# Expert weights made one burst later, gate copies right behind their products, gate rows loaded five ahead, list prices of 1.7 and 1.8

## The chip, the cores and the metric

The kernel runs on one core of a Trainium2 chip. The metric is device time in microseconds. Before the change the median of 3 runs is 2131.26 us (2128.56 to 2132.33). One more execution was taken with the hardware profiler on; all rows below are of that one.

## The reference

One decoder layer on 256 tokens of width 2048, in float32: a token mixer (RG-LRU and Mamba-2 heads), and then PEER, the channel mixer, where the change lies. Both halves are modulated by six vectors made from `c` and `w_ada`; the sixth, `gate2`, scales the output of PEER.

```
def peer(h, w_q, sub_keys, u_tab, v_tab):
    q = (h @ w_q) as 8 heads x 2 halves x 128
    sub = q . sub_keys                       # 128 keys for each half
    sub_val, sub_idx = top_k(sub, 16)        # for each half
    cand = sub_val[0][:, None] + sub_val[1]  # 16 x 16 sums for each head
    top_val, top_pos = top_k(cand, 16)       # 16 experts of 128 * 128 for each head
    gate = softmax(top_val)
    act = gelu(x . u_tab[expert])
    return sum(gate * act * v_tab[expert])

x = x + gate2 * peer(rms_norm(x) * (1 + scale2) + shift2)
out = rms_norm(x, final_norm_g)
```

Each token picks 128 of 16384 experts. `u_tab` and `v_tab` have 16384 rows of 2048 floats (8 KB).

## The kernel before

The part before about 770 us (projections, scans, output projection) is not touched. PEER is then done in four ways at once, under an order that the program writes out by hand.

**U items.** An expert index is split as j * 128 + i. For j below 100, products with all rows of `u_tab` are made: 25 quads of four j, each in 8 items, so 200 items, numbered 0 to 199 here (`it` in `u_quad`). An item takes one 512 KB load of `u_tab` (tile `raw`, 4 buffers, issued by SP), a copy to float32r on ACT (L149, tile `hl`, 4 buffers), the remainder of that copy on DVE (L158), and 12 matmuls on PE (L1499 to L1501). SP issues the next load of `raw` only when L158 has freed a buffer. The products go to two arrays in DRAM (`ads2`, tile name `ad`).

**Lists.** While the items run, list products (`l_step`, L1426) sort the picks with j below 100 into lists of 32 tokens by 116 places: 16 products for tokens 0 to 127, then `l_dec(0)` and `open_sparse`, then 16 for the other tokens, and `l_dec(1)`. Each product needs one-hot operands that `prep` makes on DVE (L1411 to L1415), at most three products ahead. Then come 32 products `g_step` (L1474), which build dense weights `Wt` for the 28 values of j from 100 up; they need `prep` as well, and two copies from PSUM to `Wt` on ACT (L1483). After `open_sparse` there is one PSUM bank for all of them. Each entry of this list has a price (1.3 for `l_step`, 1.5 for `g_step`); every item pays in 1.0, and an entry is issued when its price is covered (`bg_pay`).

**Sparse quads.** For the lists, 58 quads of 4 x 128 places are done (`v_quad`, L1590). A quad needs 4 gathers of up to 128 rows of `v_tab` (`v_feed`, L1549, up to 1 MB each, into tiles `tk`, `vq`, `vx`: 6 row buffers, 8 later) and 4 gathers of 128 single floats from `ads2` (`w_feed`, L1562, into `lsm`). POOL issues all of them, in order. From the floats `w_make` makes the quad's weights `Wz`: a GELU on ACT (L1576) and three operations on DVE (L1577, L1579, L1580). `tick` is called once an item: it feeds, makes weights, and issues a quad when the quads are behind an even spread to the end.

**Gate rows.** `gate2` takes 64 loads of 256 KB of `w_ada` (L1341, tile `two`, 2 buffers), each added by one DVE operation (L1354, L1356). `gate2_tick` is called at every second item from 22 on, and at every item from 160 on; not between the start of the lists and `open_sparse` (`sq["first"]`).

**The end.** After item 199 come 56 items for the 28 dense j (L454, L456: U side) and 56 items of V (L1690), with the quads spread between them, then two sums over rows, the final norm and the output.

What a tick issues is fixed when the program is built. An engine takes its instructions in that order: a GELU on ACT whose floats have not landed holds every later copy on ACT, and a gate operation on DVE whose load has not landed holds every later L158.

Of the kernel before, what the change touches and what calls it, by code (L numbers as in the profile page):

```python
# [23 lines left out]
JD = 28  # L24
# [39 lines left out]
def hybrid_kernel(ctx, tc, xT, cols, w_ada, w_in, lru_w, w_o1, w_o2, w_q, keys, u_t, v_t, fng, out):  # L64
# [1270 lines left out]
    def gate2_load():  # L1335
        n = gt["ld"]
        gt["ld"] += 1
        if n < 64:
            q, k = divmod(n, 16)
            gt[n] = ads[:, 2 * (n % 2):2 * (n % 2) + 2].rearrange("p a b -> p (a b)")  # L1340
            sp.dma_start(gt[n], w_ada[k * 128:(k + 1) * 128, 5 * D + q * 512:5 * D + (q + 1) * 512])  # L1341

    def gate2_tick():
        n = gt["n"]
        q, k = divmod(n, 16)
        if n >= 64 or sq["first"] or (k == 0 and gt["fin"] < q - 1):
            return
        if n == 0:
            gate2_load()
        gate2_load()  # L1350
# [69 lines left out]
    def l_step(tb, n):  # L1420
# [16 lines left out]
        return l_pe, l_ew, 1.3  # L1437
# [28 lines left out]
    def g_step(n):  # L1466
        P = {}

        def g_pe():
            a, o = gpend.pop(0)  # L1470
            P[0] = pv = gbank()[:, :NG * JD].rearrange("p (t j) -> p t j", t=NG)
            for t in range(NG):
                for i in range(2):
                    pe.matmul(pv[:, t], a[:, t], o[:, t, i], start=(i == 0), stop=(i == 1))  # L1474

        def g_ew():
            if not Wt:
                Wt.extend(pr.tile([128, JD // 2, 256], FT, name="Wt", tag=f"W{b}") for b in range(2))
            if n < 29:
                prep()  # L1480
            for b in range(2):
                j = slice(b * JD // 2, (b + 1) * JD // 2)
                act.activation(Wt[b][:, :, n * NG:(n + 1) * NG].rearrange("p j t -> p t j"), P[0][:, :, j],  # L1483
                               AF.Copy, scale=1.0 / GSCALE)
        return g_pe, g_ew, 1.5
# [5 lines left out]
    def u_quad(n, pay):  # L1491
        ps = [bank((2 * n + tb) % 3) for tb in range(2)]
        for kp in range(8):
# [29 lines left out]
            if it >= 22 and it % 2 == 0 or it >= 160:  # L1523
                gt["slot"] = it
                gate2_tick()
# [43 lines left out]
    def w_make():  # L1569
        q = sq["made"]  # L1570
        if q >= NQD or q > sq["n"] + 1 or sq["w"] < 4 * q + 4 or sq["it"] < wt[q] + 3:
            return
# [9 lines left out]
    def v_quad(q):  # L1582
# [10 lines left out]
        if m == b - 1:  # L1593
            if b == GA:
                for c in range(4):
# [5 lines left out]
    def sparse():  # L1601
# [3 lines left out]
        while sq["made"] <= q:  # L1605
            sq["it"] += 3
# [15 lines left out]
    def open_sparse():  # L1622
        gbk[:] = [3]
        sq.update(on=True, first=False, all=8 * NU - sq["at"] - 1 + 4 * JD)
        for _ in range(6):
            w_feed(1)
            v_feed(1)
# [262 lines left out]
```

## Time and profile before

| | us |
|---|---|
| median of 3 runs | 2131.26 |
| the profiled execution, its own time | 2114.3 |
| its span, first to last instruction | 2112.6 |
| PE busy | 1982.3 (94%) |
| DVE busy | 1416.3 (67%) |
| ACT busy | 895.7 (42%) |
| POOL busy | 764.6 (36%) |
| moved by DMA | 642.20 MB, mean 304 GB/s |

In the rows below a time is in microseconds from the start of the span, "mean ns" is the mean of one instruction, and a bracket behind a row of the timeline is the idle time of the engine just before it, with what ended that. "PEclk" is the granted clock of TensorE, 1.00 at full speed. "DMA share" is the mean busy share of the 16 DMA engines; it comes out a little above 1 where they are all busy. In the time of the lists PE does an item in about 3 us.

### The profile page before, as it was taken

How to read it: one execution, taken by the hardware profiler on the slowest of the kernel's cores; microseconds unless marked ns; L12 is line 12 of the kernel's file. 1: busy time of each engine (PE TensorE's matmuls, PEld its weight loads, DVE VectorE, ACT ScalarE, POOL GpSimd, SP SyncE). 2: the span in 40 equal slices, each digit the busy share in tenths (PEclk: the TensorE clock that was granted, in tenths of full speed). 3: DMA queues.
4: the chain of work that ended last, by engine and by line, in shares of the span. 5: the costliest groups of instructions: out<-in, count | busy, mean ns of one | idle time of the engine just before them, and what ended most of it. 6: DMA issues, size and time to landing. Idle time of an engine off the chain costs nothing. (4 is left out here: it accounts for less than half of the span.)

```text
span 2112.6 us, 33462 instructions
## 1 busy us (share of the span) xinstructions
PE 1982.3 (94%) x12488; PEld 1552.0 (73%) x12488; DVE 1416.3 (67%) x2177; ACT 895.7 (42%) x1364; POOL 764.6 (36%) x637
## 2 busy tenths in 40 slices
PE   7999999999999999999989779888899999999897
PEld 4789999989998898888777555555565766656563
DVE  3368888898878769779979767565533444445444
ACT  3346666677634454444443222323222333333232
POOL 0013344322202110002301545555456666666463
PEclk9999999999999999999999899999999999999899
DMA  9967667777899855677665799999899899989994
GB/s 388 406 228 252 230 228 236 245 262 267 269 323 331 312 175 178 209 235 265 229 227 186 262 371 379 396 328 339 330 369 415 335 420 422 421 302 422 373 419 175
DMA packets 257356, 642.20 MB, mean 304 GB/s; under 512 B 28352, under 2 KB 132976, under 8 KB 230000
## 3 DMA queue, kind: packets, MB, share of 16 engines
q1 hardware_dynamic: 205712, 390.38, 53.3%
q0 software_dynamic: 40832, 215.51, 25.3%
q10 hardware_dynamic: 10640, 34.08, 4.3%
q8 instruction: 100, 1.64, 0.3%
q14 instruction: 72, 0.59, 0.1%
HBM read 650.45 MB, written 17.34 MB: 316 GB/s over the span
## 5 line engine op out<-in xcount | busy, mean ns | idle before, releaser
L149 ACT ACTIVATE hl<-raw 128x1024 fp32r<-128x1024 f32 x554 | 585.1, 1059 | 1038.7 <-PE b L1501 295.1
L158 DVE TENSOR_TENSOR hl<-raw,hl 128x1024 fp32r<-128x1024 f32 x554 | 699.8, 1270 | 134.7 <-ACT hl L149 133.7
L454 PE MATMUL b<-H,hl 128*128 128x512 f32 x1056 | 377.6, 401 | 1.1 <-ACT X L675 1.1
L1499 PE MATMUL b<-hl,H 128*128 128x512 f32 x800 | 326.5, 408 | 0.5 <-ACT X L1505 0.5
L1501 PE MATMUL b<-hl,H 128*128 128x512 f32 x800 | 317.9, 397 | 2.1 <-DVE hl L158 2.1
L1500 PE MATMUL b<-hl,H 128*128 128x512 f32 x800 | 317.6, 397 | 0.0
L1562 POOL DMA_INDIRECT lsm<-ad,X x232 | 267.0, 1151 | 131.0 <-issue 68.8
L456 PE MATMUL b<-H,hl 128*128 128x256 f32 x1056 | 295.6, 280 | 2.4 <-DVE hl L158 2.4
L454 PEld LDWEIGHTS b<-H,hl 128*128 128x128 f32 x1056 | 198.2, 188 | 61.4 <-issue 12.1
L1549 POOL DMA_INDIRECT tk<-in_v_t,X x132 | 155.2, 1176 | 160.9 <-PE b L1590 104.8
L456 PEld LDWEIGHTS b<-H,hl 128*128 128x128 f32 x1056 | 199.2, 189 | 4.0 <-DVE hl L158 3.0
L1499 PEld LDWEIGHTS b<-hl,H 128*128 128x128 f32 x800 | 153.8, 192 | 50.5 <-issue 20.1
L1501 PEld LDWEIGHTS b<-hl,H 128*128 128x128 f32 x800 | 153.6, 192 | 37.6 <-DVE hl L158 3.6
L1500 PEld LDWEIGHTS b<-hl,H 128*128 128x128 f32 x800 | 154.0, 192 | 29.9
L1690 PE MATMUL b<-hl,X 128*128 128x512 f32 x672 | 162.4, 401 | 9.4 <-DVEq L1806 5.7
L1590 PE MATMUL b<-tk,Wz 128*32 128x512 f32 x1056 | 160.2, 616 | 10.5 <-DMA tk<-in_v_t,X 10.5
L1690 PEld LDWEIGHTS b<-hl,X 128*128 128x128 f32 x672 | 128.0, 193 | 50.3 <-issue 18.3
L809 PE MATMUL b<-H,hl 128*128 128x256 f32 x560 | 161.7, 289 | 0.4 <-DVE ggt L466 0.4
L811 PE MATMUL b<-H,hl 128*128 128x256 f32 x560 | 158.4, 283 | 1.3 <-DVE hl L158 1.3
L810 PE MATMUL b<-H,hl 128*128 128x256 f32 x560 | 158.4, 283 | 0.0
L1579 DVE SCALAR_TENSOR_TENSOR lsm<-lsm,LG 128x4 f32<-128x4 f32 x58 | 9.7, 168 | 209.3 <-ACT lsm L1576 209.2
L394 DVE SCALAR_TENSOR_TENSOR adacc<-adr,cact,adacc 128x1024 f32<-128x1024 f32 x90 | 124.3, 1381 | 25.4 <-DMA adr<-in_w_ada 25.3
(383 smaller groups left out, 3340.5 us busy)
## 6 DMA issues: line engine op xcount, KB each, us to landing
raw<-in_u_t SPq DMA_DIRECT2D x228, 512.0 KB, 5.1
raw<-in_w_in SPq DMA_DIRECT2D x146, 512.0 KB, 4.9
adr<-in_w_ada SPq DMA_DIRECT2D x96, 512.0 KB, 5.0
adw<-in_w_ada SPq DMA_DIRECT2D x64, 512.0 KB, 10.2
raw<-in_w_o SPq DMA_DIRECT2D x64, 512.0 KB, 6.0
raw<-in_w_q SPq DMA_DIRECT2D x32, 512.0 KB, 4.5
two<-in_w_ada SPq DMA_DIRECT2D x64, 256.0 KB, 7.3
raw<-in_u_t ACTq DMA_DIRECT2D x28, 512.0 KB, 7.9
```

What stands on the lines that cost most here:

```text
L149: act.activation(t[:, 0], r, AF.Copy)
L158: dve.tensor_sub(t[:, 1], r, t[:, 0].bitcast(FT))
L454: pe.matmul(ps, w[:, 0, c], x[:, k].rearrange("p a b -> p (a b)"), start=(k == first), stop=False, skip_group_check=True)
L456: pe.matmul(ps[:, :256], w[:, 1, c], x[:, k, 0], start=False, stop=(k == 15), skip_group_check=True)
L809: pe.matmul(ps, wh, hT[:, k, 0, :], start=(k == 0), stop=False)
L810: pe.matmul(ps, wh, hT[:, k, 1, :], start=False, stop=False)
L1499: pe.matmul(o, hh, w[:, 0, :, kk], start=(k == 0), stop=False)
L1500: pe.matmul(o, hl_, w[:, 0, :, kk], start=False, stop=False)
L1501: pe.matmul(o, hh, w[:, 1, :, kk], start=False, stop=(k == 15))
L1562: pool.indirect_dma_start(wA[:, n % 32:n % 32 + 1], None, adf[i], bass.IndirectOffsetOnAxis(ap=LW[:, tb, g, m:m + 1], axis=0), bounds_chec ...
L1590: pe.matmul(sb[c][32 * g:32 * g + 32, :], Wz[:, q % NW, g], buf[4 * q + g][:, c * 512:(c + 1) * 512], start=(m == a), stop=(m == b - 1), s ...
L1690: pe.matmul(ob[tb * 2 + c], w[:, i, s], v[:, k, c * 512:(c + 1) * 512], start=(jj == 0 and (i, k) == (0, 0)), stop=(jj == JD - 1 and k == 1))
```

## The change

Five edits.

1. `w_make` makes a quad's weights only when the quad before it has been issued (`q > sq["n"]` in place of `q > sq["n"] + 1`), and not before 6 ticks after their floats were asked for (3 before).
2. `open_sparse` issues 8 gathers of floats first, and then rows and floats in turn, rows first.
3. `g_step` issues the two copies to `Wt` directly behind the products, not one item later.
4. Gate rows get 6 buffers (two in `two`, four in `S0`) and are loaded five ahead. Their ticks go on in the time of the lists, at every fourth item; after it they come at every second item to the end. All 64 are done before `S0` takes the sums of the first 14 quads.
5. Prices: 1.7 for `l_step` (1.3), 1.8 for `g_step` (1.5).

```diff
-            gt[n] = ads[:, 2 * (n % 2):2 * (n % 2) + 2].rearrange("p a b -> p (a b)")
+            i = n % 6
+            gt[n] = (ads[:, 2 * i:2 * i + 2].rearrange("p a b -> p (a b)") if i < 2 else
+                     S0[:, (i - 2) * 512:(i - 1) * 512])
...
-        if n >= 64 or sq["first"] or (k == 0 and gt["fin"] < q - 1):
+        if n >= 64 or (k == 0 and gt["fin"] < q - 1):
             return
-        if n == 0:
+        while gt["ld"] < n + 6:
             gate2_load()
-        gate2_load()
...
-        return l_pe, l_ew, 1.3
+        return l_pe, l_ew, 1.7
...
         def g_pe():
+            if not Wt:
+                Wt.extend(pr.tile([128, JD // 2, 256], FT, name="Wt", tag=f"W{b}") for b in range(2))
             a, o = gpend.pop(0)
-            P[0] = pv = gbank()[:, :NG * JD].rearrange("p (t j) -> p t j", t=NG)
+            pv = gbank()[:, :NG * JD].rearrange("p (t j) -> p t j", t=NG)
             for t in range(NG):
                 for i in range(2):
                     pe.matmul(pv[:, t], a[:, t], o[:, t, i], start=(i == 0), stop=(i == 1))
+            for b in range(2):
+                j = slice(b * JD // 2, (b + 1) * JD // 2)
+                act.activation(Wt[b][:, :, n * NG:(n + 1) * NG].rearrange("p j t -> p t j"), pv[:, :, j],
+                               AF.Copy, scale=1.0 / GSCALE)
...
-        return g_pe, g_ew, 1.5
+        return g_pe, g_ew, 1.8
...
-            if it >= 22 and it % 2 == 0 or it >= 160:
+            if it >= 22 and it % (4 if sq["first"] else 2) == 0:
...
-        if q >= NQD or q > sq["n"] + 1 or sq["w"] < 4 * q + 4 or sq["it"] < wt[q] + 3:
+        if q >= NQD or q > sq["n"] or sq["w"] < 4 * q + 4 or sq["it"] < wt[q] + 6:
...
         sq.update(on=True, first=False, all=8 * NU - sq["at"] - 1 + 4 * JD)
+        w_feed(8)
         for _ in range(6):
+            v_feed(1)
             w_feed(1)
-            v_feed(1)
```

Counted in the built programs, by the item behind which a thing is issued:

| | before | after |
|---|---|---|
| `open_sparse` | 109 | 116 |
| `l_dec(1)` | 132 | 145 |
| gate loads issued by then | 31 of 64 at item 108 | 42 of 64 at item 108 |
| first quad | 115 | 122 |
| quads issued by item 126 | 4 | 2 |
| quads issued by item 200 | 25 | 23 |
| first product of `g_step` | 136 | 149 |
| last product of `g_step` | 182 | after 199 (three together at the end of the U items) |
| last gate operation | 166 | 163 |

On POOL, at `open_sparse`, the order before is as follows: `lsm` is a gather of 128 floats, `tk`, `vq` and `vx` are gathers of rows.

```order
129 L1539 MEMSET vx 128x2048
130 L1562 DMA lsm<-ad_8715,X_8024 128x1
131 L1549 DMA tk<-in_v_t,X_8024 128x2048
132 L1562 DMA lsm<-ad_8715,X_8024 128x1
133 L1549 DMA tk<-in_v_t,X_8024 128x2048
134 L1562 DMA lsm<-ad_8715,X_8024 128x1
135 L1549 DMA tk<-in_v_t,X_8024 128x2048
136 L1562 DMA lsm<-ad_8715,X_8024 128x1
137 L1549 DMA tk<-in_v_t,X_8024 128x2048
```

And after:

```order
129 L1538 MEMSET vx 128x2048
130 L1561 DMA lsm<-ad_8715,X_8024 128x1 x8
131 L1548 DMA tk<-in_v_t,X_8024 128x2048
132 L1561 DMA lsm<-ad_8715,X_8024 128x1
133 L1548 DMA tk<-in_v_t,X_8024 128x2048
134 L1561 DMA lsm<-ad_8715,X_8024 128x1
135 L1548 DMA tk<-in_v_t,X_8024 128x2048
136 L1561 DMA lsm<-ad_8715,X_8024 128x1
137 L1548 DMA tk<-in_v_t,X_8024 128x2048
```

The floats of the first two quads now stand ahead of all rows, where before three gathers of rows stood ahead of the fourth of floats.

On DVE, from the end of `l_dec(0)` to the first weights, before (L1356 is a gate operation, L1411 to L1415 are one `prep`, L1577 to L1580 the weights `Wz`):

```order
1184 L1464 TENSOR_TENSOR LG<-b_10635,LG 128x116
1185 L1356 SCALAR_TENSOR_TENSOR adgx<-two,cact,adgx 128x512
1186 L158 TENSOR_TENSOR hl<-raw,hl 128x1024 x2
1187 L1411 TENSOR_TENSOR two<-lists 128x1024
1188 L1413 TENSOR_TENSOR lists<-lists 128x232
1189 L1415 TENSOR_TENSOR lists<-lists 128x928
1190 L1356 SCALAR_TENSOR_TENSOR adgx<-two,cact,adgx 128x512
1191 L1577 TENSOR_TENSOR Wz<-lsm,LC 128x128
1192 L1579 SCALAR_TENSOR_TENSOR lsm<-lsm,LG 128x4
1193 L1580 TENSOR_TENSOR Wz<-Wz,lsm 128x128
```

And after, with the gate rows partly in `S0`:

```order
1208 L1416 TENSOR_TENSOR lists<-lists 128x928
1209 L1357 SCALAR_TENSOR_TENSOR ohr<-S_8026,cact,ohr 128x512
1210 L158 TENSOR_TENSOR hl<-raw,hl 128x1024 x2
1211 L1412 TENSOR_TENSOR two<-lists 128x1024
1212 L1414 TENSOR_TENSOR lists<-lists 128x232
1213 L1416 TENSOR_TENSOR lists<-lists 128x928
1214 L1357 SCALAR_TENSOR_TENSOR ohr<-S_8026,cact,ohr 128x512
1215 L1576 TENSOR_TENSOR Wz<-lsm,LC 128x128
1216 L1578 SCALAR_TENSOR_TENSOR lsm<-lsm,LG 128x4
1217 L1579 TENSOR_TENSOR Wz<-Wz,lsm 128x128
```

The first weights stood two copies L158 behind `l_dec(0)`; now they stand five behind it.

On ACT, at the end of the program, before (L1576 is the GELU of a quad's floats, L1731 the square root of the final norm, L1722 squares of the sums):

```order
1058 L1722 ACTIVATE b_23063,rf<-H 128x512
1059 L1722 ACTIVATE b_23064,rf<-H 128x512
1060 L1576 ACTIVATE lsm<-lsm 128x4
1061 L1731 ACT_TABLE_LOAD
1062 L1731 ACTIVATE rf<-rf,epsc 128x1
1063 L1737 ACTIVATE H<-H,rf 128x1024
1064 L1722 ACTIVATE b_17410,rf<-H 128x512
```

And after:

```order
1052 L1575 ACTIVATE lsm<-lsm 128x4
1053 L1732 ACT_TABLE_LOAD
1054 L1732 ACTIVATE rf<-rf,epsc 128x1
1055 L1738 ACTIVATE H<-H,rf 128x1024
1056 L1575 ACT_TABLE_LOAD
1057 L1575 ACTIVATE lsm<-lsm 128x4
1058 L1723 ACTIVATE b_17425,rf<-H 128x512
1059 L1723 ACTIVATE b_17426,rf<-H 128x512
1060 L1723 ACTIVATE b_17427,rf<-H 128x512
1061 L1723 ACTIVATE b_17428,rf<-H 128x512
1062 L1732 ACT_TABLE_LOAD
```

The GELU of the last quad moved behind the first final norm, with two more table loads.

## Rows read from the trace of the kernel before

**Rows 1.** Busy time by stretch. The columns are the stretch, its length, the busy time of PE, its weight loads, DVE, ACT and POOL with instruction counts, the granted clock, the DMA share and GB/s.

```profile
1172.00:1210.00 38.00, 25.32 (x143) 18.36 (x145) 23.00 (x43) 10.08 (x13) 26.37 (x24) 0.82 0.79 288
1210.00:1255.00 45.00, 40.85 (x248) 26.69 (x240) 30.49 (x39) 10.28 (x14) 30.00 (x25) 1.00 1.02 391
1255.00:1275.00 20.00, 12.24 (x73) 7.86 (x74) 15.11 (x20) 4.17 (x6) 2.53 (x3) 0.74 0.69 240
1275.00:1370.00 95.00, 84.34 (x576) 56.86 (x576) 63.05 (x102) 27.25 (x47) 54.48 (x46) 0.98 1.03 402
1370.00:1510.00 140.00, 120.27 (x867) 78.11 (x867) 81.71 (x118) 41.81 (x80) 71.61 (x59) 0.95 0.90 328
1510.00:1640.00 130.00, 118.77 (x684) 75.77 (x683) 44.71 (x60) 36.66 (x57) 77.29 (x68) 0.96 1.01 388
...
1125.00:1172.00 47.00, 47.00 (x265) 37.52 (x265) 45.75 (x53) 18.09 (x19) 7.09 (x4) 1.00 0.60 191
...
1680.00:1850.00 170.00, 168.76 (x1072) 117.11 (x1070) 73.97 (x124) 60.50 (x102) 112.36 (x96) 1.00 1.02 421
```

**Rows 2.** Waits of PE between 1175 and 1275: who waited for what, microseconds in total, times, the longest.

```profile
PE b L1426 <- DVE lists L1415: 22.4, 5, 10.0
```

**Rows 3.** The same between 1275 and 1560.

```profile
PE b L1474 <- ACT Wt L1483: 24.9, 13, 3.9
PE b L1474 <- ACT lsm L1576: 5.3, 3, 2.1
...
PE b L1367 <- ACT Wt L1483: 1.6, 1, 1.6
PE b L1367 <- ACT lsm L1576: 1.6, 1, 1.6
```

**Rows 4.** Timeline of ACT and then of DVE and PE behind `open_sparse`.

```profile
1193.76 1.28 ACT L1576 ACT_TABLE_LOAD   x1 [11.95 <-DMA lsm<-ad,X]
...
1195.29 0.17 DVE L1579 SCALAR_TENSOR_TENSOR lsm<-lsm,LG 128x4 f32<-128x4 f32 x1 [11.91 <-ACT lsm L1576]
...
1199.64 0.93 PE L1426 MATMUL b<-lists,two 128*128 128x116 f16 x8 [10.03 <-DVE lists L1415]
```

**Rows 5.** Timeline of POOL at the same place: the first gathers of floats and of rows, the fourth and the sixth of rows.

```profile
1176.62 1.20 POOL L1562 DMA_INDIRECT lsm<-ad,X  x1 [43.81 <-DVE ohr L1461]
1178.13 1.43 POOL L1549 DMA_INDIRECT tk<-in_v_t,X  x1 [0.30 <-issue]
...
1187.59 0.99 POOL L1549 DMA_INDIRECT tk<-in_v_t,X  x1 [0.30 <-issue]
...
1192.79 0.99 POOL L1549 DMA_INDIRECT vx<-in_v_t,X  x1 [0.31 <-issue]
```

**Rows 6.** Timeline around one late gate row: DVE, then ACT, then PE.

```profile
1483.22 0.75 DVE L1356 SCALAR_TENSOR_TENSOR adgx<-two,cact,adgx 128x512 f32<-128x512 f32 x1 [6.77 <-DMA two<-in_w_ada]
...
1496.09 1.06 ACT L149 ACTIVATE hl<-raw 128x1024 fp32r<-128x1024 f32 x1 [5.09 <-DMA raw<-in_u_t]
1497.06 0.54 ACT L1483 ACTIVATE Wt<-b 128x112 f32<-128x112 f32 x2
...
1497.65 0.55 PE L1474 MATMUL b<-ohr,two 128*128 128x28 f16 x16 [3.92 <-ACT Wt L1483]
```

**Rows 7.** Timeline of PE around a wait of 2.07 us, and two matmuls of an item behind it.

```profile
1467.33 0.55 PE L1474 MATMUL b<-ohr,two 128*128 128x28 f16 x16 [2.07 <-ACT lsm L1576]
...
1468.74 0.63 PE L1499 MATMUL b<-hl,H 128*128 128x512 f32 x1
1469.17 0.63 PE L1500 MATMUL b<-hl,H 128*128 128x512 f32 x1
...
1474.46 0.39 PE L1500 MATMUL b<-hl,H 128*128 128x512 f32 x1
1474.69 0.39 PE L1501 MATMUL b<-hl,H 128*128 128x512 f32 x1
```

**Rows 8.** Timeline of PE in the time of the lists: list products two items and one item apart.

```profile
1135.45 0.59 PE L1426 MATMUL b<-lists,two 128*128 128x116 f16 x8
...
1141.42 0.59 PE L1426 MATMUL b<-lists,two 128*128 128x116 f16 x8
...
1144.68 0.59 PE L1426 MATMUL b<-lists,two 128*128 128x116 f16 x8
```

**Rows 9.** Waits of DVE between 1275 and 1560.

```profile
DVE lsm L1579 <- ACT lsm L1576: 46.7, 12, 6.0
...
DVE adgx L1356 <- DMA two<-in_w_ada: 22.0, 8, 6.8
DVE ohr L1356 <- DMA two<-in_w_ada: 11.6, 3, 5.9
```

**Rows 10.** The end of the program: timeline of ACT, and the last quad on PE.

```profile
2089.78 1.28 ACT L1731 ACT_TABLE_LOAD   x1
...
2104.18 0.60 ACT L1722 ACTIVATE b<-H 128x512 f32<-128x512 f32 x1 [0.61 <-DVE H L1719]
2104.71 0.19 ACT L1722 ACTIVATION_READ_ACCUMULATOR b<-H 128x1 f32 x1
2105.39 0.29 ACT L1731 ACTIVATE rf<-rf,epsc 128x1 f32<-128x1 f32 x1 [0.49 <-DVE rf L1730]
...
2097.58 0.62 PE L1590 MATMUL b<-vq,Wz 128*32 128x512 f32 x2 [2.35 <-DMA vq<-in_v_t,X]
```

More of the change, by code (lines that the diff above doesn't have):

```diff
@@ L1466, in g_step @@
     def g_step(n):
-        P = {}
         def g_pe():
+            if not Wt:
+                Wt.extend(pr.tile([128, JD // 2, 256], FT, name="Wt", tag=f"W{b}") for b in range(2))
             a, o = gpend.pop(0)
-            P[0] = pv = gbank()[:, :NG * JD].rearrange("p (t j) -> p t j", t=NG)
+            pv = gbank()[:, :NG * JD].rearrange("p (t j) -> p t j", t=NG)
             for t in range(NG):
@@ L1474, in g_pe @@
                     pe.matmul(pv[:, t], a[:, t], o[:, t, i], start=(i == 0), stop=(i == 1))
+            for b in range(2):
+                j = slice(b * JD // 2, (b + 1) * JD // 2)
+                act.activation(Wt[b][:, :, n * NG:(n + 1) * NG].rearrange("p j t -> p t j"), pv[:, :, j],
+                               AF.Copy, scale=1.0 / GSCALE)
         def g_ew():
-            if not Wt:
-                Wt.extend(pr.tile([128, JD // 2, 256], FT, name="Wt", tag=f"W{b}") for b in range(2))
             if n < 29:
                 prep()
[L1481 to L1484, printed above, removed]
-        return g_pe, g_ew, 1.5
+        return g_pe, g_ew, 1.8
     dram = ctx.enter_context(tc.tile_pool(name="ad", bufs=1, space=bass.MemoryType.DRAM))
@@ L1594, in v_quad @@
             if b == GA:
+                assert gt["n"] == 64
                 for c in range(4):
@@ L1605, in sparse @@
         while sq["made"] <= q:
-            sq["it"] += 3
+            sq["it"] += 6
             w_feed()
```

## Prediction

> **What bounds the kernel now.** I read the busy time by stretch first, then who PE waits for, then timelines where those waits are longest. Up to 1172 PE is hardly ever idle: in 1125 to 1172 it is busy for all 47 us, with the DMA engines at a share of 0.60 [rows 1]. Behind `open_sparse` this turns round: the DMA share goes to 1.02 or 1.03 whenever nothing stands still, and PE gets holes: 25.3 us of 38, 12.2 of 20, 120.3 of 140 [rows 1]. From 1680 to 1850 both are full, PE at 168.8 of 170 and DMA at 1.02 [rows 1]. So from about 1172 to the end two things are at their limit together: PE by its instructions, DMA by its bytes. Neither PE's work nor the bytes change with this edit. A stall costs time only as far as it leaves the DMA engines without work, and this is what I add up.
>
> The stalls have three causes. (a) A GELU waits for its floats. At 1193.76 ACT had been held 11.95 us by the first floats, DVE was held 11.91 us behind it, and PE 10.03 us behind the next `prep` [rows 4]. The fourth gather of floats was issued behind three of rows [rows 5]. It goes on later: DVE waits 46.7 us for GELUs from 1275 to 1560 [rows 9]. (b) A gate operation waits for its load, 33.6 us of DVE in the same stretch [rows 9]. At 1483.22 it had waited 6.77 us; L158 behind it freed a buffer late, so `raw` was late (5.09 us on ACT), and PE stood 3.92 us [rows 6]. (c) A product of `g_step` waits for the copies of the last one, 24.9 us in 13 waits and 5.3 us more behind a GELU [rows 3]: the copies stand behind the split of the next item, and that split waits for the matmuls which PE has just done.
>
> In PE's own waits that is 22.4 us [rows 2] and 33.4 us [rows 3].
>
> **What the change takes away.** (a) With the floats of two quads ahead of all rows, and 6 ticks and one quad of distance, no GELU should find its floats missing; the 10.03 us goes, and the same kind of wait later. (b) With loads five ahead a gate row has about ten items to land, 30 us, against two items before; the DVE waits of 33.6 us go. (c) The copies now run as soon as the products are done, while PE does the next item (2.7 us, below). ACT waits there for 0.55 us of products, after a split that had waited for the same matmuls, so the wait moves behind it and costs nothing while `raw` is in time. If `raw` is late, ACT is held at L149 as before and the next product waits again.
>
> How much time these stalls cost follows from the DMA engines. Taking 1.02 as full, a stretch loses its length times (1.02 - share) / 1.02 [rows 1]:
>
> - 1172 to 1210: 38 x 0.23 / 1.02 = 8.6 us
> - 1255 to 1275: 20 x 0.33 / 1.02 = 6.5 us
> - 1370 to 1510: 140 x 0.12 / 1.02 = 16.5 us
> - 1510 to 1640: 130 x 0.01 / 1.02 = 1.3 us
> - the stretches at 1.02 and 1.03: none
>
> That is 32.9 us of the DMA engines, the most that edits 1 to 3 can bring while the bytes bind. It is less than the 55.8 us of PE waits, since part of those lies under transfers that had to be made anyway.
>
> **What it adds and moves.**
>
> *The later opening.* The list price of 1.7 puts `open_sparse` 7 items later. An item takes 2.71 us and a list product 0.55 (5.97 us for two items and one product, 3.26 us for one of each [rows 8]), so at 1.7 an item is 2.71 + 0.55 / 1.7 = 3.03 us and seven are 21.2 us. PE does useful items in that time; the DMA engines run at 0.60 in place of 1.02 [rows 1] and lose 21.2 x 0.42 / 1.02 = 8.7 us.
>
> *Floats first.* An issue on POOL takes 1.3 us (four of them from 1187.59 to 1192.79 [rows 5]). Eight of floats put the first rows 10.4 us behind the first floats, against 1.5 us before [rows 5]: 8.9 us later, at the share of the list time, 3.7 us. The fourth gather of rows is then issued 10.4 + 3 x 2.6 = 18 us after the start, and the first quad, six items behind (18 us), may wait on it by one landing. That wait is no second loss: the DMA engines are busy in it.
>
> *What remains of the stalls.* I leave a quarter of the 17.8 us from 1370 on, 4.5 us: `raw` still shares the engines with the bursts of rows. Both ends are open here, nothing and all 17.8 us, since no row shows this stretch without late gates and floats. I take a quarter because the timeline [rows 6] leads the largest hole back to a gate row.
>
> *Gate loads.* 42 are out by item 108, where 31 were: 11 x 262 KB = 2.9 MB leave the full stretch for one with room; at the 402 GB/s of 1275 to 1370 [rows 1] that is 7.2 us gained. On SP they stand in front of `raw` by 0.5 us of issue; the burst of six at item 21 lies in a stretch where PE had cover. On DVE one operation of 0.75 us each fourth item joins the lists [rows 6], while a `prep` is needed at 1 / 1.7 of the items in place of 1 / 1.3; that relieves DVE by more than it adds.
>
> *The end of the U items.* Three products of `g_step` come together there, some 3 us of PE with copies between; DMA runs on beside, so 0, and 3 us if it does not.
>
> *The tail.* The last GELU now stands between the two final norms on ACT, with a table load of 1.28 us each way [rows 10]. The first load hides in the wait for the last rows (the last quad starts at 2097.58, after 2.35 us of waiting [rows 10]). The second begins when the squares end, 2104.71 + 0.19 = 2104.9, and ends 1.28 us later at 2106.2, where the square root began at 2105.39 [rows 10]: 0.8 us lost. [...] The row shows a load of 1.28 us with nothing behind it but work, so the sum keeps 0.8.
>
> *The clock.* Behind a PE wait of 2.07 us matmuls are 0.43 us apart instead of 0.23 for some 3 us [rows 7], so short waits cost double on PE. [...]
>
> **The sum.** Lost before 32.9; lost after 8.7 + 3.7 + 4.5 = 16.9; difference 16.0, plus 7.2 of gate loads, less 0.8 at the tail: 22.4 us. The profiled execution would go from 2114.3 to 2091.9 us. The median of the runs is higher, 2131.26, by a factor of 1.008; scaled by it the gain is 22.6 us and the time 2108.7, say 2109 us.
>
> **Rivals.**
>
> *PE's waits are the time (faster by far).* If DMA has more room than the share tells, all 55.8 us of PE waits go [rows 2, 3], with a few us of half clock behind them, say 4: some 60 us, 2071 us. For it: from 1370 to 1510 the share is 0.90 at 328 GB/s, when 1.02 gives 421 later [rows 1]. Against it: 1275 to 1370 is full at 1.03 with PE at 84.3 of 95, so there the bytes came first [rows 1].
>
> *The burst that opens late (slower).* Two more quads are still to be done at item 126, and the stretch from 1680 on has no room on either engine [rows 1]. If the stalls of the middle stay because `raw` and the bursts keep starving each other, then the loss is 8.7 + 3.7 of the opening and 3 for the left-over products, less 7.2: 8 us slower, with the tail 9, so 2140 us. It decides once more than about 28 of the 32.9 us remain. For it: two of the three holes begin with a wait for `raw` or a gate row behind a burst. Against it: the float and gate waits that start them are what is taken away.
>
> *The first wait changes its name (no change).* The 10 us at the opening come back as a wait of the first quad for its rows, the copies are held by late `raw` as often as before, and gain and loss cancel: 2131 us.
>
> **How the numbers follow.** The sum above holds with a chance of 0.66, with its own range of 2095 to 2122 (no stalls left, 4.5 us better; the middle not improved, 13 us worse). PE's waits as the time 0.16; no change 0.08; slower 0.10. A measurement here can tell 0.2%, 4 us, from nothing. The main case and the first rival are faster: 0.82. For 8 in 10 I go down to the first rival, nearly, and up to just beyond no change: 2076 to 2132 us.
>
> **What would show it.** Right: no GELU wait of 12 us on ACT behind `open_sparse`; DVE's waits on gate rows gone; the waits of L1474 on `Wt` down from 24.9 to a few us; the DMA share from the opening to the end of the U items near 1.0 throughout; the U items ending some 20 us earlier. Wrong: a long wait of the first quad on rows, `raw` waits as long as before, or holes of DMA share in the last stretch that were not there. If PE's holes close without the DMA share reaching 1.02, the first rival is right.

## The result, and the profile after

| | before | after |
|---|---|---|
| median, us | 2131.80 (2128.56 to 2132.49, 4 runs) | 2104.36 (2100.41 to 2109.80, 4 runs) |
| ratio to before | 1 | 0.9876 [0.9848, 0.9904] |
| the profiled execution, its own time | 2114.3 | 2109.8 |
| its span | 2112.6 | 2108.1 |

The changed kernel is 27.4 us faster; 2109 us was predicted, 4.6 us above what came. The profiled execution of before ran 17 us below the median of its kernel, so the two traces lie only 4.5 us apart. Both kernels were therefore traced once more (E1 and E5 below), and where a size matters both traces of each are used.

Busy time of the changed kernel in the stretches of [rows 1], same columns:

```profile
1125.00:1172.00 47.00, 47.00 (x254) 37.78 (x253) 44.06 (x52) 18.39 (x20) 7.08 (x4) 1.00 0.67 217
1172.00:1210.00 38.00, 37.72 (x201) 30.29 (x200) 36.05 (x52) 16.14 (x19) 12.00 (x8) 1.00 0.71 229
1210.00:1255.00 45.00, 33.04 (x166) 16.97 (x166) 19.97 (x29) 8.90 (x12) 32.61 (x30) 0.81 0.92 340
1255.00:1275.00 20.00, 20.00 (x120) 12.68 (x119) 15.21 (x20) 4.52 (x6) 14.83 (x12) 1.00 1.03 406
1275.00:1370.00 95.00, 84.75 (x518) 52.55 (x516) 57.23 (x92) 25.42 (x38) 53.77 (x45) 0.95 1.04 402
1370.00:1510.00 140.00, 128.64 (x875) 81.46 (x876) 80.41 (x114) 44.07 (x80) 79.18 (x67) 0.95 0.92 348
1510.00:1640.00 130.00, 115.98 (x803) 73.45 (x798) 57.22 (x84) 39.16 (x72) 77.17 (x64) 0.95 0.98 377
1680.00:1850.00 170.00, 163.57 (x1013) 112.34 (x1015) 72.42 (x122) 57.62 (x97) 106.27 (x93) 0.98 1.02 422
```

The hole of PE at the opening (25.3 busy of 38) is gone. A new one stands 40 us later, in 1210 to 1255: 33.0 of 45, at a granted clock of 0.81. In 1370 to 1510 PE gained 8 us, and the DMA share rose only from 0.90 to 0.92. From 1275 to 1370 the DMA engines are full in both traces, at shares of 1.03 and 1.04 and 402 GB/s: the bytes bind there. In the second trace of before (E1) they were at 0.91 in that stretch.

The new hole is the first quads. Timeline of PE in the changed kernel:

```profile
1219.19 1.89 PE L1589 MATMUL b<-tk,Wz 128*32 128x512 f32 x2 [7.19 <-DMA tk<-in_v_t,X]
1224.22 1.92 PE L1589 MATMUL b<-tk,Wz 128*32 128x512 f32 x2 [3.14 <-DMA tk<-in_v_t,X]
1227.19 1.92 PE L1589 MATMUL b<-tk,Wz 128*32 128x512 f32 x2 [1.06 <-DMA tk<-in_v_t,X]
```

and the GELU that stood 11.95 us in [rows 4], on ACT:

```profile
1209.97 1.28 ACT L1575 ACT_TABLE_LOAD   x1
1211.27 0.20 ACT L1575 ACTIVATE lsm<-lsm 128x4 f32<-128x4 f32 x1
```

No bracket: its floats were there. In their place the first quads wait for rows, 11.4 us in three waits, since these now leave POOL behind eight gathers of floats (in E7, where they do not, the first quad does not wait for rows).

Waits of PE between 1275 and 1560, the view of [rows 3], and then those of DVE, the view of [rows 9], both in the changed kernel:

```profile
PE b L1475 <- ACT Wt L1478: 7.1, 1, 7.1
PE b L1589 <- DMA tk<-in_v_t,X: 5.8, 5, 2.1
PE b L1589 <- DVE Wz L1579: 4.9, 1, 4.9
PE b L1368 <- DVE LG L1465: 3.3, 1, 3.3
```

```profile
DVE lsm L1578 <- ACT lsm L1575: 43.2, 8, 10.6
DVE hl L158 <- ACT hl L149: 39.5, 17, 6.9
```

No gate row is waited for there any more (33.6 us in [rows 9]). DVE still waits 43.2 us for GELUs, where [rows 9] had 46.7. The 13 waits on copies to `Wt` have become one, of 7.1 us. This is what makes it, ACT and then PE:

```profile
1414.01 1.06 ACT L149 ACTIVATE hl<-raw 128x1024 fp32r<-128x1024 f32 x1 [7.73 <-DMA raw<-in_u_t]
1414.97 0.54 ACT L1478 ACTIVATE Wt<-b 128x112 f32<-128x112 f32 x2
...
1415.56 0.58 PE L1475 MATMUL b<-ohr,two 128*128 128x28 f16 x16 [7.07 <-ACT Wt L1478]
```

ACT takes the split of the next item before the copies, and stood 7.73 us for `raw` there. The name of the wait is the copy; its cause is the load. Such waits have grown. ACT waiting for `raw` from 1175 to 1640, before and then changed:

```profile
ACT hl L149 <- DMA raw<-in_u_t: 47.9, 9, 11.4
```

```profile
ACT hl L149 <- DMA raw<-in_u_t: 75.8, 16, 11.7
```

In the second traces it is 58.6 us (E1) and 84.8 us (E5). ACT itself is no limit there (busy for 44.07 and 44.89 of the 140 us from 1370 to 1510 in the two traces of the changed kernel), but the loads are later against the work that needs them than they were.

### The profile page after: what moved, and what is told of

The parts are those of the page before. It is cut to its first block, busy times and chain, and to the rows that moved or that the text cites. A ratio compares the mean times of both kernels' runs of the same rounds, so it can differ in the third digit from the quotient of the medians.

```text
span 2108.1 us, 33475 instructions
## 1 busy us (share of the span) xinstructions
PE 1985.3 (94%) x12488; PEld 1545.1 (73%) x12488; DVE 1421.7 (67%) x2177; ACT 899.1 (43%) x1366; POOL 766.8 (36%) x637
## 5 line engine op out<-in xcount | busy, mean ns | idle before, releaser
L149 ACT ACTIVATE hl<-raw 128x1024 fp32r<-128x1024 f32 x554 | 585.2, 1059 | 1018.7 <-PE b L1500 242.1
L158 DVE TENSOR_TENSOR hl<-raw,hl 128x1024 fp32r<-128x1024 f32 x554 | 703.7, 1276 | 169.7 <-ACT hl L149 141.6
L454 PE MATMUL b<-H,hl 128*128 128x512 f32 x1056 | 378.9, 402 | 1.1 <-ACT X L675 1.1
L1498 PE MATMUL b<-hl,H 128*128 128x512 f32 x800 | 320.6, 401 | 0.9 <-ACT X L1504 0.5
L1500 PE MATMUL b<-hl,H 128*128 128x512 f32 x800 | 312.8, 391 | 2.0 <-DVE hl L158 2.0
L1499 PE MATMUL b<-hl,H 128*128 128x512 f32 x800 | 312.2, 390 | 0.0
L1589 PE MATMUL b<-tk,Wz 128*32 128x512 f32 x1056 | 239.9, 642 | 29.8 <-DMA tk<-in_v_t,X 21.2
L454 PEld LDWEIGHTS b<-H,hl 128*128 128x128 f32 x1056 | 199.1, 188 | 62.2 <-issue 12.8
L1548 POOL DMA_INDIRECT tk<-in_v_t,X x132 | 148.8, 1127 | 162.8 <-PE b L1589 123.8
L1589 PE MATMUL b<-vq,Wz 128*32 128x512 f32 x536 | 195.0, 614 | 4.6 <-DMA vq<-in_v_t,X 4.0
L1498 PEld LDWEIGHTS b<-hl,H 128*128 128x128 f32 x800 | 150.6, 188 | 50.5 <-issue 19.9
L1500 PEld LDWEIGHTS b<-hl,H 128*128 128x128 f32 x800 | 150.5, 188 | 35.7 <-DVE hl L158 2.9
L1499 PEld LDWEIGHTS b<-hl,H 128*128 128x128 f32 x800 | 150.9, 189 | 29.0
L1589 PEld LDWEIGHTS b<-tk,Wz 128*32 128x32 f32 x1056 | 53.3, 116 | 143.1 <-issue 95.5
```

Of the source, the lines that this page charges most:

```text
L149: act.activation(t[:, 0], r, AF.Copy)
L158: dve.tensor_sub(t[:, 1], r, t[:, 0].bitcast(FT))
L454: pe.matmul(ps, w[:, 0, c], x[:, k].rearrange("p a b -> p (a b)"), start=(k == first), stop=False, skip_group_check=True)
L1498: pe.matmul(o, hh, w[:, 0, :, kk], start=(k == 0), stop=False)
L1499: pe.matmul(o, hl_, w[:, 0, :, kk], start=False, stop=False)
L1500: pe.matmul(o, hh, w[:, 1, :, kk], start=False, stop=(k == 15))
```

## Experiments

**How they are read.** There are four sets of runs: the one of the result, E1 to E4, E5 to E8, and E9 to E12. Each has its own runs of before, and their medians differ: 2131.8, 2118.9, 2132.4 and 2114.5 us. E9 to E12 ran on another chip than E1 to E8. So kernels are compared by their ratio to before in the same set. Expectations given in microseconds were written for the scale of the result, where before takes 2131.8 us. The changed kernel ran in two sets, at 0.9876 and 0.9859; 0.987 is taken for it, and 0.1% is 2.1 us. It did not run in the sets of E1 to E4 and E9 to E12, so a comparison with it there assumes that the ratio carries over. I come back to that.

One table for all traces, worked out from timelines and stretches. Times are us. "Opening" is the first gather of floats, counted from the first product of item 0; "U items" is from there to the first product of the dense j (L454); "rest" runs from that to the end of the span. "Lost" is length times (1.02 - DMA share) / 1.02 from 330 us behind the first product of item 0 to L454; "MB" is what is moved from the same mark to 15 us before the end. The views round share and GB/s, so "lost" is good to some 2 us and "MB" to some 0.5.

| kernel | opening | U items after it | rest | item 0 to end | lost | MB |
|---|---|---|---|---|---|---|
| before | 333 | 446 | 490 | 1269 | 31 | 339.2 |
| E1 before again | 333 | 454 | 489 | 1277 | 40 | 339.1 |
| changed | 352 | 414 | 499 | 1264 | 30 | 335.4 |
| E5 changed again | 351 | 402 | 506 | 1259 | 25 | 335.4 |
| E2 old prices | 336 | 414 | 496 | 1246 | 17 | 337.1 |
| E3 old gates | 351 | 424 | 496 | 1272 | 39 | 338.4 |
| E4 old copies | 351 | 408 | 500 | 1259 | 29 | 335.3 |
| E6 old weights | 352 | 404 | 502 | 1257 | 25 | 335.7 |
| E7 old floats | 351 | 415 | 498 | 1264 | 34 | 335.5 |
| E8 gates alone | 337 | 443 | 497 | 1277 | 40 | 337.5 |
| E9 old weights and floats | 351 | 402 | 496 | 1249 | 25 | 335.3 |
| E10 old list price | 337 | 414 | 494 | 1245 | 17 | 337.5 |
| E11 old prices and weights | 336 | 410 | 490 | 1235 | 12 | 336.5 |
| E12 gates every second | 340 | 411 | 489 | 1240 | 21 | 335.7 |

Two traces of one kernel differ by 8 to 12 us in "U items" and by 5 to 7 us in the sum, so smaller differences in the table say nothing.

**E1, before once more.** No edit.

> The kernel before, unchanged, timed and profiled once more, since its profiled execution (2114.3 us) lies 17 us under the median of its other runs (2131.8) while that of the changed kernel (2109.8) does not. All theories: median 2131 us, within 0.2% of before. If a profiled execution again comes out near 2114, profiling or the execution itself varies by that much and only medians may be compared; if it comes out near 2131, its trace is the one to compare with.

Measured: 2116.98 us, ratio 0.9996 [0.997, 1.0021]. The trace has a span of 2127.0 us, nearer to the runs of the result. Waits of PE between 1175 and 1640:

```profile
PE b L1474 <- ACT Wt L1483: 21.8, 13, 2.1
PE b L1426 <- DVE lists L1415: 17.3, 4, 10.0
PE b L1367 <- DVE LG L1464: 11.0, 1, 11.0
PE b L1367 <- DVE adgx L1356: 7.8, 1, 7.8
```

The first two are those of [rows 2, 3] again. The third, the gate sums waiting for the end of the lists (`l_dec`), is 0.5 to 12.4 us in the fourteen traces, and no experiment aims at it. The last one is not in the trace of before that the prediction was made from: L1367 sums the gate columns on PE, and stood for the gate operation itself. Timeline of DVE, and then of PE, there:

```profile
1504.64 0.75 DVE L1356 SCALAR_TENSOR_TENSOR adgx<-two,cact,adgx 128x512 f32<-128x512 f32 x1 [2.04 <-DMA two<-in_w_ada]
...
1505.54 1.84 PE L1367 MATMUL b<-ones,adgx 128*128 128x1 f32 x8 [7.80 <-DVE adgx L1356]
```

Late gate rows thus reach PE on a second way, besides late `raw`. The median is within 0.1% of before in its set, as expected, but 15 us below that of the result: the sets differ.

**E2, the old prices** in the changed kernel.

```diff
-        return l_pe, l_ew, 1.7
+        return l_pe, l_ew, 1.3
...
-        return g_pe, g_ew, 1.8
+        return g_pe, g_ew, 1.5
```

> The changed kernel with the list prices of before (1.3 and 1.5), so that the lists open at item 109 or so. Theory D (time is DMA time lost, so what counts is how early the row gathers start): the 8.7 us that the later opening costs come back, 2093 to 2098 us. Rival P (time is what PE waits for the lists and for the copies to Wt, and the slower pace is what took those waits away): the waits return, 2112 to 2125 us.

Measured: 2085.78 us, ratio 0.9837 [0.9807, 0.9867]: 0.3% or 7 us below the changed kernel, near the 8.7 us of theory D, with intervals that overlap. The trace says more, 13 to 18 us from item 0 to the end. The middle, 1370 to 1510, in this kernel and then in the changed one (E5):

```profile
1370.00:1510.00 140.00, 131.17 (x970) 85.17 (x961) 89.86 (x128) 50.29 (x95) 85.56 (x71) 0.99 0.98 369
```

```profile
1370.00:1510.00 140.00, 128.22 (x898) 82.01 (x900) 81.83 (x116) 44.89 (x80) 80.58 (x68) 0.98 0.94 358
```

And the late part, waits of PE in V, first changed, then old prices:

```profile
PE b L1691 <- DVEq L1807: 10.8, 1, 10.8
PE b L1691 <- ACT X L447: 4.1, 1, 4.1
...
PE b L1691 <- DVE X L448: 3.6, 1, 3.6
PE b L1589 <- DVE Wz L1579: 3.1, 2, 1.7
```

```profile
PE b L1691 <- ACT X L447: 5.0, 1, 5.0
PE b L1691 <- DVEq L1807: 4.6, 1, 4.6
```

The first row is the wait at the start of the second half of V, for a register that a guard of the program loads (L1807). It is 10.1 to 11.9 us in all seven traces with the list price 1.7, and 4.1 to 5.7 us in all seven with 1.3; the wait of 3.6 us on L448 goes with it (at most 0.9 with 1.3). These 9 us stand 750 us behind the place that the price moves. Timeline of PE there, changed, and then the old prices:

```profile
1950.64 5.73 PE L1691 MATMUL b<-hl,X 128*128 128x512 f32 x24
1967.18 4.87 PE L1691 MATMUL b<-hl,X 128*128 128x512 f32 x12 [10.81 <-DVEq L1807]
```

```profile
1951.30 13.61 PE L1691 MATMUL b<-hl,X 128*128 128x512 f32 x48 [4.59 <-DVEq L1807]
```

From the end of the first half of V to the start of the second PE does no V for 10.1 to 11.9 us, in all fourteen traces. In the seven with 1.3 one quad (32 matmuls) stands in this gap and fills 5 to 7 us of it; in the seven with 1.7 none does. So the price does not make the gap; it moves the quad that filled it.

**E3, the old gate rows** in the changed kernel: two buffers, one load ahead, no ticks in the time of the lists, every item from 160 on.

```diff
...
-        if n >= 64 or (k == 0 and gt["fin"] < q - 1):
+        if n >= 64 or sq["first"] or (k == 0 and gt["fin"] < q - 1):
             return
-        while gt["ld"] < n + 6:
+        if n == 0:
             gate2_load()
+        gate2_load()
...
-            if it >= 22 and it % (4 if sq["first"] else 2) == 0:
+            if it >= 22 and it % 2 == 0 or it >= 160:
```

> The changed kernel with the gate rows of before: two buffers, one load ahead, none in the time of the lists, every item from 160 on. Theory D: 7 us of gate bytes return to the full stretch and about half of the holes of the DMA share (8 us) come back: 2112 to 2122 us. Rival P: gate rows hold DVE alone and PE only at times: 2104 to 2109 us.

Measured: 2110.81 us, ratio 0.9969 [0.9945, 0.9994]. This interval and that of the changed kernel don't touch: by the ratio 1.0%, some 21 us, of the gain hang on the gate rows, more than the 8 to 18 us of theory D; by the trace it is 8 to 13 us (1272 against 1264 and 1259). E4, which ran in the same set and keeps the gate rows, took 10 us less. In the trace the waits are back, on DVE and on PE (1175 to 1640):

```profile
DVE adgx L1356 <- DMA two<-in_w_ada: 48.3, 10, 9.0
DVE ohr L1356 <- DMA two<-in_w_ada: 38.3, 7, 8.5
```

```profile
PE b L1367 <- DVE LG L1464: 12.4, 1, 12.4
...
PE b L1367 <- DVE adgx L1356: 10.1, 1, 10.1
```

The waits of DVE for gate rows are longer than in the kernel before, 93 us with the 6.4 at L1354, against 63 us in E1 over the same stretch. 338.4 MB are left at the mark in place of 335.4.

**E4, the old copies** in the changed kernel: both copies to `Wt` one item behind the products.

```diff
-            for b in range(2):
-                j = slice(b * JD // 2, (b + 1) * JD // 2)
-                act.activation(Wt[b][:, :, n * NG:(n + 1) * NG].rearrange("p j t -> p t j"), pv[:, :, j],
-                               AF.Copy, scale=1.0 / GSCALE)
+            P[0] = pv
...
```

(the same lines then stand at the end of `g_ew`).

> The changed kernel with the two copies to Wt one item later, as before. Theory D: at 1.8 few products stand one item apart, and DMA goes on beside a PE wait of 1.6 us: within 4 us of the changed kernel, 2101 to 2109 us. Rival P: most of the 24.9 us of waits of L1474 return, 2120 to 2130 us.

Measured: 2100.99 us, ratio 0.9916 [0.9887, 0.9944]. By the ratio the copies are worth 0.5%, 10 us, more than the 4 us that theory D allows and less than rival P asked for. By the trace nothing is lost: 1259 us from item 0 to the end, as in E5. Waits of PE, 1175 to 1640:

```profile
PE b L1593 <- DMA tk<-in_v_t,X: 14.5, 9, 7.6
PE b L1477 <- ACT Wt L1486: 13.5, 7, 5.3
...
PE b L1477 <- ACT lsm L1579: 3.6, 2, 2.1
```

17.1 us behind ACT, against 11.4 and 7.9 us on `Wt` in the two traces of the changed kernel: 6 to 9 us more, and less waiting for rows (14.5 against 21.2 and 19.1). Without gate rows in front of it, the old place costs far less than the 30.2 us of [rows 3].

**E5, the changed kernel once more.**

> The changed kernel, unchanged, timed beside the kernel before once more, so that the parts undone can be set against it on equal terms. Both theories: ratio 0.985 to 0.990 of the kernel before, as in its first measurement (0.9876).

Measured: 2102.74 us, ratio 0.9859 [0.9828, 0.989], as expected; span 2104.1.

**E6, the old rule for weights.**

```diff
-        if q >= NQD or q > sq["n"] or sq["w"] < 4 * q + 4 or sq["it"] < wt[q] + 6:
+        if q >= NQD or q > sq["n"] + 1 or sq["w"] < 4 * q + 4 or sq["it"] < wt[q] + 3:
...
-            sq["it"] += 6
+            sq["it"] += 3
```

(The second change belongs to edit 1 too: when a quad has to be issued and its weights are not made, the count of ticks is put forward by the same number.)

> The changed kernel with the weights of a quad made as before (up to two quads ahead, 3 ticks after their floats are asked for). Theory D (the GELU waits hold ACT, then raw, then the DMA engines): some holes come back, 5 to 10 us slower than the changed kernel, ratio to before 0.990 to 0.993. Rival F (the floats sent ahead at the opening and the early gate rows did the work, the later weights do nothing or cost at the end, where quads waited for Wz): same or up to 5 us faster than the changed kernel, ratio 0.985 to 0.988.

Measured: 2103.43 us, ratio 0.986 [0.9827, 0.9894]. No difference, as rival F said. In its trace the first GELU waits 5.4 us for floats on ACT.

**E7, rows and floats in turn from the first gather.**

```diff
-        w_feed(8)
         for _ in range(6):
-            v_feed(1)
             w_feed(1)
+            v_feed(1)
```

> The changed kernel with the gathers at the opening in the order of before (one of floats, one of rows, in turn, no eight of floats first). Theory D: rows start 9 us earlier, so 3.7 us of DMA time come back, and with 6 ticks of distance the first GELU does not wait: 3 to 4 us faster, ratio 0.983 to 0.987. Rival F: the first GELU waits again for floats behind rows and the 10 us stall returns: 5 to 10 us slower, ratio 0.990 to 0.993.

Measured: 2107.19 us, ratio 0.988 [0.9845, 0.9915]: between the forecasts, and within the interval no difference. In its trace the first GELU waits 3.2 us for floats, and the first quad 4.4 us for its weights and not for rows.

**E8, the gate rows alone:** edit 4 put into the kernel before, the reverse of E3.

> The kernel before with the gate rows of the change alone (six buffers, five ahead, every fourth item in the time of the lists, every second item after). Theory D: the bytes moved early (7 us) and the holes behind late gate rows (about half of 18 us) give 10 to 16 us, ratio 0.992 to 0.995. Rival P: the waits for floats and for the copies remain and fill the place, 0 to 5 us, ratio 0.998 to 1.000.

Measured: 2120.43 us, ratio 0.9934 [0.9909, 0.996]: 0.7%, 14 us, alone, as theory D said. Its one trace doesn't show them (1277 us from item 0). On PE the other stalls are still there, 20.1 us on `Wt` and 13.8 us on the lists (21.8 and 17.3 in E1).

**E9, weights and floats both undone** (the diffs of E6 and E7 together).

> The changed kernel with edits 1 and 2 both undone (weights made for two quads ahead after 3 ticks, rows and floats in turn from the first gather); gates, copies and prices stay. Undone singly, neither moved the time beyond its measurement (0.986 and 0.988 of before). Theory D (the two edits are substitutes: either alone keeps the first GELU from standing in front of floats that have not landed): with both undone the GELU stall of some 12 us at the opening returns on ACT, PE waits there for a prep again, and later GELU waits with it; DMA time lost by it 5 to 10 us, ratio to before 0.990 to 0.993. Rival N (with gate rows never late and copies in place the stall at the opening lies under transfers that had to be made anyway): the stall returns in the trace, but the time stays, ratio 0.985 to 0.988.

Measured: 2096.53 us, ratio 0.9907 [0.9881, 0.9932], the number that theory D asked for: 0.4%, 8 us. The trace shows its stall, ACT and then PE:

```profile
1218.64 1.28 ACT L1575 ACT_TABLE_LOAD   x1 [12.61 <-DMA lsm<-ad,X]
...
1221.85 0.79 PE L1500 MATMUL b<-hl,H 128*128 128x512 f32 x1 [7.72 <-DVE hl L158]
...
1226.12 3.64 PE L1589 MATMUL b<-tk,Wz 128*32 128x512 f32 x32
```

But its first quad (last row) no longer waits for rows: 7.7 us of PE here against 11.4 us there, and 1249 us from item 0 to the end. In the trace one wait stands in place of the other, as rival N said. Ratio and trace disagree, and the 8 us are not settled.

**E10, only the list price back to 1.3.**

```diff
-        return l_pe, l_ew, 1.7
+        return l_pe, l_ew, 1.3
```

> The changed kernel with the price of l_step alone put back from 1.7 to 1.3; g_step stays at 1.8. The opening comes at item 109, as before; the last product of g_step at item 182 or later. With both prices put back the ratio to before was 0.984. Theory D (the later opening alone is what the prices cost): ratio 0.982 to 0.985, opening near 1183 us, U items ended near 1597. Rival G (the price of g_step matters as much, by products left over at the end of the U items): ratio 0.986 to 0.988, as the changed kernel.

Measured: 2084.27 us, ratio 0.986 [0.9825, 0.9895]. The interval holds both forecasts. The trace is that of E2 in each column, with 4.3 us at L1807 and no wait on L448: what the prices do to the trace, the list price does alone.

**E11, old prices and old weights** (the diffs of E2 and E6).

> The changed kernel with edits 5 and 1 undone (prices 1.3 and 1.5, weights made for two quads ahead after 3 ticks): what the runs so far say is the better mix. Theory D: the earlier opening gives its 5 to 8 us, and at the tail the GELU of the last quad stands ahead of the final norm again, so the two more table loads and the waits of the last quad on its weights go, 1 to 3 us: ratio 0.981 to 0.985. Rival W (making weights later is what lets the first GELU find its floats when the opening is early): a GELU stall comes back at the opening and the ratio is 0.985 to 0.988.

Measured: 2089.17 us, ratio 0.987 [0.9839, 0.99]. That is rival W's number, but not its mechanism: at the opening ACT stood for floats 3.85 us in this trace, not 12. It has the shortest sum of the table, 1235 us, in one trace that ran 9 us below its own median. Not better than E2.

**E12, E11 with gate ticks at every second item in the lists too.**

```diff
-            if it >= 22 and it % (4 if sq["first"] else 2) == 0:
+            if it >= 22 and it % 2 == 0:
```

> The kernel of the run before this one, with gate ticks at every second item also in the time of the lists (every fourth there before); the last gate operation comes some 15 items earlier. Theory D (gate bytes are best moved where the DMA engines have room, ahead of the opening): some ten more loads of 262 KB leave the full stretch, up to 6 us gained, ratio 0.980 to 0.984. Rival V (in the time of the lists DVE is as full as PE, 45.75 us of 47, so each further gate operation of 0.75 us makes a prep late and PE waits at the list products): PE waits at L1426 grow by 5 to 10 us, ratio 0.985 to 0.990.

Measured: 2082.84 us, ratio 0.9844 [0.9815, 0.9874]: between the forecasts. The time of the lists, 1100 to 1180, in E11 and then in E12:

```profile
1100.00:1180.00 80.00, 76.29 (x425) 60.74 (x425) 77.75 (x104) 28.81 (x31) 7.94 (x5) 0.99 0.61 194
```

```profile
1100.00:1180.00 80.00, 75.38 (x408) 59.67 (x406) 78.12 (x96) 27.08 (x29) 7.07 (x4) 0.98 0.62 201
```

DVE is busy for 77.8 and 78.1 of 80 us, so each added gate operation pushes something out; the opening comes 3.7 us later (340 against 336), for 0.8 MB less behind the mark, 2 us at 402 GB/s. Waits for the operands of the lists grew by 0.5 us, where rival V asked for 5 to 10. E2 and E12 have the lowest ratios, 0.9837 and 0.9844; against 0.987 both intervals overlap with the changed kernel's, so neither is shown to beat it.

**Do the ratios add up?** Gate rows 0.99% (undone) or 0.66% (alone), copies 0.46%, weights and floats together 0.37%, prices -0.33%: 1.2 to 1.5%, where the whole is 1.3%. If only the kernel before had drifted between sets and all others not, own times would have to be compared with some 2103.5 us: gate rows 7, copies -3, weights and floats -7, prices -18 us, which adds up to a loss of some 20 us where 27 were gained. That speaks for the ratios. It is no proof, with single terms good to about 0.4%; a run of the changed kernel in the sets of E1 and E9 would have settled it.

## Why the prediction was right, and where not

*What bounds it, and the sign: right.* The kernel gained 1.3%, close to the 22.4 us of the sum, and PE and DMA are still both near their limit late in the program (1680 to 1850: PE busy for 163.6 of 170 us, a DMA share of 1.02). But the parts of the sum were not of the sizes that I gave them, and the near hit is in part luck.

*Gate rows: right, with one way missed.* The waits on gate rows went (33.6 us to none). The sum gave this edit 7.2 us for bytes and most of the 13.3 us that were to go from 1370 on, as the timeline [rows 6] led there; E3 and E8 give 21 and 14 us by their ratios, the largest part of the whole. Their traces show less: 8 to 13 us in E3, none in E8. Bytes: E3 against the changed kernel shows 3.0 MB, as forecast (2.9 MB). What I missed is that L1367 waits for the gate operation directly, 7.8 us in E1 and 10.1 us in E3; the one profiled execution of before had no such row, and it was one of the shorter ones.

*The GELU at the opening: right that it goes, and the place it goes to was named.* ACT did not wait there. "The first quad may wait on it by one landing" came as 11.4 us, which I put at nothing because the DMA engines would be busy. Between 1210 and 1255 they were at 0.92 and 0.93 in the two traces, so 4 us were lost. The sum had 8.6 + 6.5 - 3.7 = 11.4 us for edits 1 and 2. What they bring together is open, between nothing (the traces) and 8 us (the ratio of E9); either alone can be left out (E6, E7). The term for the floats was too small: the first rows leave POOL 15.0 us behind the first floats (1195.86 to 1210.81), 1.9 us for each of the eight, where the sum had 10.4 us at 1.3. E7, with rows first again, was not faster, so this lateness is not seen in the time.

*"It goes on later": misread.* The prediction took the 46.7 us that DVE waits for GELUs from 1275 to 1560 [rows 9] for floats that had not landed. In the trace of before a GELU waited for floats three times, 18.8 us in all, and 17.8 of them at the first two. Between 1275 and 1560 ACT never waited for floats: where its waits there have a name, it stood for the matmuls of PE (125.2 us at L149) or for `raw` (13.6 us), nearly always at the copy L149 in front of the GELU. So the later weights had nothing to take away there, and DVE's wait stayed at 43.2 us (27.2 in E5).

*Copies: waits right, worth open.* 24.9 us in 13 waits became 7.1 us in one (up to 1640: 11.4 us in three, and 7.9 in two in E5), and the longest is the case the prediction kept open, ACT held by late `raw`. The forecast that these waits lie under transfers agrees with the trace of E4 and not with its ratio.

*"I leave a quarter of the 17.8 us", 4.5 us: this term failed.* At the measured shares, 140 x 0.10 / 1.02 = 13.7 and 130 x 0.04 / 1.02 = 5.1 us remain, 18.8 us, as much as before; in E5 they are 11.0 and 2.5 us. So "the DMA share near 1.0 throughout" was not met. From the table, the time lost up to L454 went from 31 and 40 us to 30 and 25, by 8 us in the mean, where the sum had 16.0. With the old list price the same stretch has a share of 0.98 (E2, E10, E11), and with the old gate rows 0.90 (E3): by these traces the gate rows cleared it in part, and most of what remained was made by the change itself, by its list price. I had charged that edit only for the time before the opening. What I put the quarter on, late gate rows as the start of the holes, left out that `raw` would be late without them: ACT waits for it longer than before (75.8 and 84.8 us against 47.9 and 58.6).

*The later opening: size right at its place, its far end missed.* Forecast 21.2 us later and 8.7 us lost. The traces show it 18 us later at a share of 0.71, 18 x 0.31 / 1.02 = 5.5 us. To this come the middle (0.94 in place of 0.98, 5.5 us) and 9 us of PE in V at L1807 and L448, 6 of them because a quad no longer fills the gap there. One quad more also falls behind L454: 23 stand in front of it in place of 24, and a quad takes PE 3.64 us (32 matmuls, E9). The sum had no term for any of this; the column "rest" is 496 to 506 us with the list price 1.7 and 489 to 497 with 1.3. E2 puts the price edit at 7 us by the ratio and 13 to 18 us by the trace; E10 gives 2 us by the ratio alone. The sign is the same in all.

*The end.* One term was missing: with edit 1 the weights of the last quads come late, 3.1 us of PE on `Wz`, in all seven traces with the new rule and in none of the seven with the old. The table loads are there as forecast. ACT at the end of the changed kernel:

```profile
2083.27 1.28 ACT L1732 ACT_TABLE_LOAD   x1
...
2086.78 1.28 ACT L1575 ACT_TABLE_LOAD   x1
...
2099.29 0.19 ACT L1723 ACTIVATION_READ_ACCUMULATOR b<-H 128x1 f32 x1
2099.49 1.28 ACT L1732 ACT_TABLE_LOAD   x1
2100.79 0.29 ACT L1732 ACTIVATE rf<-rf,epsc 128x1 f32<-128x1 f32 x1
```

From the last squares (2099.48) to the square root 1.31 us pass, against 0.49 us in [rows 10]: 0.8 us, the forecast. The switch costs the 1.28 us of the load and no more that the rows show: the load ends at 2100.77, and the square root starts at 2100.79.

*Altogether* the sum missed a gain and some losses that cancel about: copies (0 in the sum, 10 us by the ratio of E4, none by its trace) on one side, and on the other the middle (9 to 14 us less cleared than forecast, by the two traces), the waits in V (9 us) and the last weights (3 us). The traces alone, 1269 and 1277 against 1264 and 1259 from item 0, would give a gain of 11 us; the medians give 27. The number came out better than the working behind it.

*The rivals.* PE's waits as the time: no, its holes closed only in part and the bytes still bind from 1255 to 1370 (DMA shares of 1.03 and 1.04). The burst that opens late: its mechanism is there (the middle did not clear, the late part grew by 9 to 17 us), but the gate rows outweighed it. The first wait changes its name: true at the opening, 10.0 us to 11.4, and not for the rest.

*The signs.* Of those for right four came: no GELU wait at the opening, no waits on gate rows, few on `Wt`, and the U items ending 24 us earlier in the mean, counted from item 0 (779 and 788 us, then 765 and 753). The DMA share near 1.0 throughout did not. Two of those for wrong came as well, the long wait of the first quad for rows and `raw` waits as long as before. So the signs don't speak for the whole working either.

## What to carry to other kernels

Loads that feed an engine on the side should be issued far enough ahead that it never stands for them: here DVE stood 33.6 us for gate rows, and what that held was everything queued behind, and that on more than one way (PE stood 3.92 us behind late `raw` in [rows 6], and 7.80 us for a gate operation in E1). When a burst is moved, read the whole program behind it, since here a quad that had filled a gap of 11 us was gone from it 750 us later. An engine that waits for an operation which itself waits in a queue does not tell which input was late (DVE waited 46.7 us for GELUs in [rows 9], and ACT never for floats in that stretch): ask the engine at the head of that queue. Take two traces of the kernel before, and a run of the reference version in every set, before terms of 5 us are added up.

## What was unexpected

The median of one and the same kernel lay at 2131.8, 2118.9, 2132.4 and 2114.5 us in four sets, while the runs of before in one set stay within some 12 us of their median; so a ratio from one set carries an error that its interval doesn't show. The gap of 10 to 12 us in front of the second half of V is there in fourteen traces, whatever the kernel; what makes the gap itself, the sums on DVE or the load of the register, was not separated. And that hole cost PE more than its length: behind the 10.81 us of idle PE there 12 matmuls took 4.87 us, 0.41 us each, at a granted clock of 0.59 (1967.2 to 1972.1), where the 24 in front of it took 5.73 us, 0.24 each, at 1.00 (1950.6 to 1956.4). In 1210 to 1255, where the first quads wait, the granted clock is 0.81, and 1.00 in the trace of before.
